# A two-layer hybrid encoder on one core: Gram and attention value products issued in uninterrupted groups, and the bank that the recurrence's chain and its read-out share

## The chip, the cores and the metric

The kernel runs on one core of a Trainium2 chip. The metric is device time in microseconds (us) of one execution; three runs of the kernel before gave 2444.28, 2445.18 and 2440.24 us, with a median of 2444.28 us. The engines are named as the profile names them: PE is TensorE's matmul, PEld its weight load, DVE VectorE, ACT ScalarE, POOL GpSimd and SP SyncE. A line such as L565 is a line of the kernel before; a line of the kernel after is said to be one.

## What is computed

The reference is two layers over a sequence of 1024 frames of width 1024. Layer 0 normalises its input, projects it once, and splits the columns: eight heads of an RWKV-7 recurrence and eight heads of banded attention, whose outputs are joined and projected back. Layer 1 is a convolution module. After each layer stands a squared-ReLU MLP of width 4096. Cut to what the change touches:

```python
def rwkv7_scan(r, decay, k, v, kk, a):          # per head, state S is 64 x 64
    def step(S, inp):
        r_t, w_t, k_t, v_t, kk_t, a_t = inp
        sa = jnp.einsum('bhij,bhj->bhi', S, -kk_t)
        S = S * w_t + sa * (kk_t * a_t) + v_t * k_t      # outer products
        return S, jnp.einsum('bhij,bhj->bhi', S, r_t)
    ...
# then, per head: y normalised, scaled, a bonus added, and times a gate g
    return (y * w + b + bonus) * g

def chunk_band_attention(q, k, v, rel_bias):    # 64-frame chunks, own and 8 previous
    s = einsum('bcqhd,bckhd->bhcqk', qc, kb) * 64 ** -0.5 + bias
    return einsum('bhcqk,bckhd->bcqhd', softmax(s), vb)

x = x + rwkv_attention_mixer(rmsnorm(x), ...)
x = x + sq_relu_mlp(rmsnorm(x), up, down)
```

## The kernel before

**Dense work.** The sequence is worked in two halves of 512 frames. Every large projection runs as split fp32r products of 128x128 by 128x512 (hi times hi, hi times lo, lo times hi), all issued by the helper `dense` at L158. In the mixer's stage these are the input projection of the first half, then of the second half, and then the output projection and the first MLP of the first half.

**The mixer.** Under that dense work lie the recurrence (`rwkv`) and the attention (`attention`), once for each half. The recurrence is worked in units of two heads by 256 frames, cut into four chunks of 64: eight units for each half, 16 in all. A unit goes through three stages, and three units are in flight at once, one in each stage:

- `prep` makes the scaled operands and the Gram products (L565): for each of four chunks and each of the two heads one product with 64 contraction rows, head 0 in rows 0 to 63 and head 1 in rows 64 to 127. The four products of a head fill one bank of tag `w`, of which there are two. L568 masks each bank into `g`. Just ahead, L552 makes the bonus sum in a `w` bank, and L554 reads it into `bv`.
- `stacks` and `invert` transpose and solve (L656, L663, L627, L639), in 64x64 products, in the one bank of tag `v`.
- `chain` carries the state over the four chunks with three dependent products each (L685, L689, L695) and reads the result out (L705, L709), all in the one bank of tag `c`; `finish` normalises it and applies the gate (L460, L467, L731), in the bank `v`.

**The attention.** For two heads and 128 queries, scores (L809, L811), a softmax, transposes of the probabilities (L831, copied to `pT` by ACT at L832), and the value products (L838): for each 128-key tile and each head one product with 64 output columns, accumulated over the key tiles. There are 32 such groups of 2 to 10 products.

**The order.** A scheduler places the instructions of each engine by their estimated readiness and a priority level: support work first, then the recurrence, then the attention, then the dense products. What is issued under the level `run` follows at once. A dense run has one head member at the dense level; the others are tied behind it at level `run`: runs of 6 in the first half of the mixer and of 12 in the second. So a mixer instruction that becomes ready waits for the dense run in hand. Each engine then carries out its own list strictly in order.

An fp32 product that is not a transpose shows up as two matmul records in the profile; a product in fp32r and a transpose show up as one. L565 thus has 256 records for 128 products, and L838 480 for 240.

Of the kernel before, what the change touches and what calls it, by code (L numbers as in the profile page):

```python
# [14 lines left out]
P = 128  # L15
# [47 lines left out]
def encoder_trunk(ctx: ExitStack, tc: tile.TileContext, x, vecs, consts, ext, w2a2, g2, w_in, w_out,  # L63
# [91 lines left out]
    def dense(*a, **k):  # L155
# [9 lines left out]
        runs["n"] += 1  # L165

    def run_of(n):
        runs.update(n=0, size=n)
# [138 lines left out]
    def load_x(h, xrp, out=None):  # L307
# [15 lines left out]
        xs, rhs = [], []  # L323
        st = Stat(pool=out, ps="c")
        for k in range(KT):
# [69 lines left out]
    def rwkv(h, rp, nbuf):  # L395
        keep = {}
        for n, w in (("xdt", C), ("wx", C + 1)):
            t = rp.tile([P, whole(NCH * w)], F32, tag=n, name=n)
            t = keep[n] = t[:, 0 : NCH * w].rearrange("p (c t) -> p c t", t=w)
            nc.gpsimd.memset(t, 0.0)  # L400
        for i in range(2):
            t = keep["xt", i] = rp.tile([P, NCH, 2, C], F32, tag=f"xt{i}", name=f"xt{i}")
            nc.gpsimd.memset(t[:], 0.0)
        units = []
        for tb in range(2 * h, 2 * h + 2):
            units += rwkv_block(tb, rp, nbuf, keep)
        n = len(units)
        for i in range(n + 2):
            gens = []
            if i >= 2:  # L410
                gens.append(units[i - 2][2]())
            if 1 <= i <= n:
                gens.append(units[i - 1][1]())
            if i < n:
                gens.append(units[i][0]())
            while gens:
                for g in list(gens):
                    try:
                        next(g)
                    except StopIteration:  # L420
                        gens.remove(g)

    def rwkv_block(tb, rp, nbuf, keep):
# [28 lines left out]
        def vbank():  # L452
            return psum("v")[:, 0:RT]

        def cbank():
            return psum("c")

# [26 lines left out]
        def prep(hp, u):  # L484
# [68 lines left out]
            bv = rp.tile([P, RT], F32, tag="bv", name="bv", bufs=nbuf)  # L553
            nc.vector.tensor_tensor(out=bv[:], in0=bps, in1=vp[:], op=ALU.mult)  # L554

# [3 lines left out]
            for q4 in range(NCH // 4):  # L559
                mb = [bank(), bank()]  # L560
                for j in range(4):
                    c = 4 * q4 + j
                    for hd in range(2):
                        s = slice(64 * hd, 64 * hd + 64)
                        nc.tensor.matmul(mb[hd][:, j * P : (j + 1) * P], bk[s, c, :], ar[s, c, :],  # L565
                                         start=True, stop=True)
                for hd in range(2):
# [107 lines left out]
        def chain(u):  # L675
# [3 lines left out]
            for hd in range(2):  # L679
                nc.vector.tensor_copy(sv[hs[hd], hd, 0, :], sfin[hs[hd], hp, :])  # L680
            cb = cbank()
            zp, up, sp = cb[:, 0:P], cb[:, 0:C], cb[:, P : 2 * P]
            own = [slice(0, C), slice(C, P)]
# [32 lines left out]
        def finish(u):  # L716
            hp, yc, bv = u["hp"], u["y"], u["bv"]
            sq = e("e3", 2)
            nc.scalar.activation(sq[:], yc[:], AF.Square)
            vq = vbank()  # L720
            rs = head_sums(vq, sq)
# [7 lines left out]
                                           op0=ALU.add, op1=ALU.add)  # L729
            gp = vbank()  # L730
            nc.tensor.matmul(gp, g2s[:, P * hp : P * hp + P], lora_in["sg"][:], start=True, stop=True)  # L731
# [19 lines left out]
    def attention(h, ap):  # L751
# [3 lines left out]
        for hp in range(4):  # L755
# [27 lines left out]
            for qi in range(4):  # L783
# [50 lines left out]
                ob = psum("a")  # L834
                for j in range(nkt):
                    for hd in range(2):
                        cs = slice(hd * C, hd * C + C)
                        nc.tensor.matmul(ob[cs, 0:P], vts[k0 + j][:, cs], pts[hd][:, j * P : (j + 1) * P],  # L838
                                         start=(j == 0), stop=(j == nkt - 1))
                yo = ap.tile([P, P], F32, tag="yo", name="yo", bufs=1)  # L840
# [350 lines left out]
```

## Time and profile before

| | |
|---|---|
| runs | 2444.28, 2445.18, 2440.24 us |
| the profiled execution's own time | 2441.99 us |
| its span | 2440.2 us |
| granted TensorE clock, mean | 0.997 |
| PE busy | 2408.0 us, 99% of the span |
| PEld busy | 1970.2 us, 81% |
| DVE busy | 1710.8 us, 70% |
| ACT busy | 1183.8 us, 49% |
| the mixer's first half on PE, beside projections | about 80 to 470 us |
| the mixer's second half, beside the first MLP | about 490 to 1060 us |

The busy time of PE joins overlapping records, whose ends are modelled. What an instruction costs PE is therefore read from the start of one row of the timeline to the start of the next.

### The profile page before, as it was taken

What the parts mean: (1) busy time and instruction counts of PE and PEld (TensorE: products, weight loads), DVE (VectorE), ACT (ScalarE), POOL (GpSimd) and SP (SyncE); (2) the same over time, 40 slices, a digit from 0 to 9 for tenths busy, and PEclk for the clock granted to TensorE, in tenths of its full rate; (3) what the DMA queues carried; (4) which work ended last, traced back from release to release, by engine and by line L of the source; (5) the groups of instructions that cost most, each with busy time, mean ns of one, the idle gap of its engine ahead of it and who ended that gap; (6) DMA issues with size and microseconds to landing.
All of it is one profiled execution on the core that took longest, in us unless ns stands there. A gap on an engine that the chain in (4) does not pass through costs nothing.

```text
span 2440.2 us, 37269 instructions
## 1 busy us (share of the span) xinstructions
PE 2408.0 (99%) x12972; PEld 1970.2 (81%) x12972; DVE 1710.8 (70%) x3561; ACT 1183.8 (49%) x2282; POOL 113.4 (5%) x251
## 2 busy tenths in 40 slices
PE   8999999999999999999999999999999999999998
PEld 6777777778888888888888888888888888888887
DVE  5688776587677675569999837699997475534434
ACT  5457656666676663443433226434333265423324
POOL 1110101100000000012000000000000000000000
PEclk9999999999999999999999999999999999999999
DMA  8654445543343322363333333433333334333332
GB/s 251 192 152 150 123 113 162 172 133 102 100 121 92 112 72 81 114 185 96 89 102 96 99 100 109 144 96 99 95 99 95 97 109 145 95 100 95 95 97 68
DMA packets 476459, 283.36 MB, mean 116 GB/s; under 512 B 44512, under 2 KB 453472, under 8 KB 476272
## 3 DMA queue, kind: packets, MB, share of 16 engines
q1 hardware_dynamic: 466080, 250.25, 35.5%
q0 software_dynamic: 9152, 29.36, 3.4%
q8 instruction: 102, 1.67, 0.3%
q10 hardware_dynamic: 1040, 1.38, 0.2%
q14 instruction: 85, 0.70, 0.1%
HBM read 247.31 MB, written 36.72 MB: 116 GB/s over the span
## 4 chain that ended last, share of the span: by engine, by line
PE 87%; DVE 4%; DMA 3%; issue 3%; ACT 2%; SPq 0%; POOL 0%; ACTq 0%; DVEq 0%; POOLq 0%
PE d L158 76%; PE w L565 1%; PE a L838 1%; PE v L639 1%; PE a L831 1%; DVE wl L236 1%; PE a L809 1%; PE c L685 1%; PE c L695 1%; DMA xd<-xo 1%; DMA pt<-pd 1%; PE a L811 1%; PE c L689 1%; DMA wr<-in_w_in_dram 0%; PE w L552 0%
## 5 line engine op out<-in xcount | busy, mean ns | idle before, releaser
L235 ACT CAST wh<-wr 128x512 fp32r<-128x512 f32 x744 | 460.3, 620 | 929.0 <-PE d L158 844.3
L158 PE MATMUL d<-xh,wh 128*128 128x512 f32 x1872 | 746.1, 399 | 1.9 <-ACT wh L235 1.3
L158 PE MATMUL d<-xh,wl 128*128 128x512 f32 x1872 | 732.3, 391 | 0.9 <-DVE wl L236 0.9
L158 PE MATMUL d<-xl,wh 128*128 128x512 f32 x1872 | 732.1, 391 | 0.0
L236 DVE TENSOR_TENSOR wl<-wr,wh 128x512 fp32r<-128x512 f32 x744 | 501.6, 684 | 196.8 <-ACT wh L235 143.0
L158 PEld LDWEIGHTS d<-xh,wl 128*128 128x128 f32 x1872 | 352.7, 188 | 77.3 <-DVE wl L236 1.6
L158 PEld LDWEIGHTS d<-xh,wh 128*128 128x128 f32 x1872 | 353.0, 189 | 73.6 <-issue 2.2
L158 PEld LDWEIGHTS d<-xl,wh 128*128 128x128 f32 x1872 | 353.2, 189 | 68.0 <-issue 0.5
L158 PE MATMUL d<-mh,wh 128*128 128x512 f32 (+1 forms) x1040 | 407.2, 392 | 0.0
L158 PE MATMUL d<-mh,wl 128*128 128x512 f32 (+1 forms) x1040 | 402.0, 386 | 0.0
L158 PE MATMUL d<-ml,wh 128*128 128x512 f32 (+1 forms) x1040 | 401.6, 386 | 0.0
L961 DVE SCALAR_TENSOR_TENSOR cv<-u,dwt,cv 128x512 f32<-128x512 f32 x480 | 332.0, 743 | 0.7
L158 PEld LDWEIGHTS d<-mh,wl 128*128 128x128 f32 x1040 | 195.3, 188 | 40.3
L158 PEld LDWEIGHTS d<-ml,wh 128*128 128x128 f32 x1040 | 195.5, 188 | 37.6
L158 PEld LDWEIGHTS d<-mh,wh 128*128 128x128 f32 x1040 | 195.4, 188 | 37.7 <-issue 0.2
L860 DVE TENSOR_TENSOR x<-d,x 128x512 f32<-128x512 f32 (+1 forms) x146 | 97.5, 678 | 153.3 <-PE d L158 152.8
L902 DVE SCALAR_TENSOR_TENSOR t<-d,rstd 128x512 f32<-128x512 f32 x128 | 86.4, 686 | 113.1 <-PE d L158 110.1
L908 DVE TENSOR_TENSOR ml<-t,mh 128x512 fp32r<-128x512 f32 x128 | 87.6, 686 | 14.0 <-ACT mh L906 11.1
L904 ACT ACTIVATE t<-t 128x512 f32<-128x512 f32 x128 | 80.0, 625 | 12.2 <-DVE t L902 11.9
L906 ACT ACTIVATE mh<-t 128x512 fp32r<-128x512 f32 x128 | 78.9, 616 | 0.0
L202 DVE TENSOR_TENSOR acc<-acc,t 128x512 f32<-128x512 f32 (+1 forms) x86 | 57.8, 673 | 11.5 <-ACT t L201 11.1
L694 ACT ACTIVATE sd<-vs,dc 64x64 f32<-64x64 f32 x128 | 44.1, 345 | 38.7 <-DVE vs L698 31.2
(265 smaller groups left out, 2355.6 us busy)
## 6 DMA issues: line engine op xcount, KB each, us to landing
wr<-in_up_dram SPq DMA_DIRECT2D x256, 256.0 KB
wr<-in_dn_dram SPq DMA_DIRECT2D x256, 256.0 KB
wr<-in_w_in_dram SPq DMA_DIRECT2D x104, 256.0 KB
wr<-in_pw_dram SPq DMA_DIRECT2D x96, 256.0 KB
wr<-in_w_out_dram SPq DMA_DIRECT2D x32, 256.0 KB
pd<-t POOLq DMA_DIRECT2D x28, 256.0 KB, 2.7
x<-xd SPq DMA_DIRECT2D x24, 256.0 KB
pt<-pd SPq DMA_DIRECT2D x42, 128.5 KB
```

The costliest lines, as they stand in the source:

```text
L158: ins = nc.tensor.matmul(*a, **k)
L202: nc.vector.tensor_tensor(out=self.acc[:, cols], in0=self.acc[:, cols], in1=sq[:, cols], op=ALU.add)
L235: nc.scalar.copy(hi[:], raw[:])
L236: nc.vector.tensor_tensor(out=lo[:], in0=raw[:], in1=hi[:].bitcast(F32), op=ALU.subtract)
L565: nc.tensor.matmul(mb[hd][:, j * P : (j + 1) * P], bk[s, c, :], ar[s, c, :], start=True, stop=True)
L694: nc.scalar.activation(sd[hs[hd], :], sv[hs[hd], hd, c, :], AF.Copy, scale=dc[hs[hd], c : c + 1])
L860: nc.vector.tensor_tensor(out=xs[m][:, cols], in0=q[:, cols], in1=xs[m][:, cols], op=ALU.add)
L902: nc.vector.scalar_tensor_tensor(out=t[:], in0=q[:], scalar=0.0, in1=rstd[:], op0=ALU.max, op1=ALU.mult)
L904: nc.scalar.activation(sq[:], t[:], AF.Square)
L906: nc.scalar.activation(hi[:], t[:], AF.Square)
L908: nc.vector.tensor_tensor(out=lo[:], in0=sq[:], in1=hi[:].bitcast(F32), op=ALU.subtract)
L961: nc.vector.scalar_tensor_tensor(out=c[:], in0=u[:, tap : tap + T], scalar=dw(tap), in1=c[:], op0=ALU.mult, op1=ALU.add)
```

## The change

It has three parts.

1. The Gram products of a unit are issued through a helper, `Visit`. Its first member carries a wait for the read of the bonus bank (`freed`, the write of `bv`); the seven others are tied behind it at level `run`. The heads alternate from product to product.
2. The attention value products of a group are issued through the same helper. The loop over key tiles and heads runs backwards, so the first product issued is the one whose transposed probabilities come last.
3. The bank of tag `c` is held by one tile for the whole half (`keep["cb"]`). The chain works in one of its first two quarters, by the parity of the head pair, with its three products in the same columns; the read-out and now also `finish` use its second half. The bank `v` is left to `stacks` and `invert`. The statistics of the second half's input go to a bank `v` in place of `c`.

```diff
+    class Visit:
+        def __init__(self, ready=None):
+            self.last, self.ready = None, ready
+
+        def __call__(self, issue, *a, **k):
+            with At("run") if self.last is not None else nullcontext():
+                ins = issue(*a, **k)
+            if self.last is None and self.ready is not None:
+                tc.add_manual_dep(ins.ins, self.ready.ins.name,
+                                  mybir.DependencyInfo(mybir.DependencyClass.Sync, mybir.DependencyReason.DATA),
+                                  reason="a visit begins when its last bank is free")
+            if self.last is not None:
+                tc.add_manual_dep(ins.ins, self.last.ins.name,
+                                  mybir.DependencyInfo(mybir.DependencyClass.NoSync, mybir.DependencyReason.DATA),
+                                  reason="one visit to an array shape")
+            self.last = ins
...
-        st = Stat(pool=out, ps="c")
+        st = Stat(pool=out, ps="v")
...
+        keep["cb"] = psum("c")
...
-            nc.vector.tensor_tensor(out=bv[:], in0=bps, in1=vp[:], op=ALU.mult)
+            freed = nc.vector.tensor_tensor(out=bv[:], in0=bps, in1=vp[:], op=ALU.mult)
...
+                visit = Visit(freed)
                 for j in range(4):
                     c = 4 * q4 + j
                     for hd in range(2):
                         s = slice(64 * hd, 64 * hd + 64)
-                        nc.tensor.matmul(mb[hd][:, j * P : (j + 1) * P], bk[s, c, :], ar[s, c, :],
-                                         start=True, stop=True)
+                        visit(nc.tensor.matmul, mb[hd][:, j * P : (j + 1) * P], bk[s, c, :], ar[s, c, :],
+                              start=True, stop=True)
...
-            cb = cbank()
-            zp, up, sp = cb[:, 0:P], cb[:, 0:C], cb[:, P : 2 * P]
+            cb = keep["cb"]
+            o = P * (hp % 2)
+            zp, up, sp = cb[:, o : o + P], cb[:, o : o + C], cb[:, o : o + P]
...
-            vq = vbank()
+            vq = keep["cb"][:, RT : 2 * RT]
...
-            gp = vbank()
+            gp = keep["cb"][:, RT : 2 * RT]
...
                 ob = psum("a")
-                for j in range(nkt):
-                    for hd in range(2):
+                visit = Visit()
+                for j in reversed(range(nkt)):
+                    for hd in (1, 0):
                         cs = slice(hd * C, hd * C + C)
-                        nc.tensor.matmul(ob[cs, 0:P], vts[k0 + j][:, cs], pts[hd][:, j * P : (j + 1) * P],
-                                         start=(j == 0), stop=(j == nkt - 1))
+                        visit(nc.tensor.matmul, ob[cs, 0:P], vts[k0 + j][:, cs], pts[hd][:, j * P : (j + 1) * P],
+                              start=(j == nkt - 1), stop=(j == 0))
```

How this moves the instructions is seen in PE's own list. In the kernel after, both helpers' products have the line L173; those written to `w` are Gram products, those to `a` value products. Other lines shift: L552, L639, L685, L731, L467, L809 and L811 become L567, L655, L702, L748, L482, L826 and L828. Rows of equal products are joined (x4).

The Gram products of the third unit of the second half, on PE. Before, from the bonus sum L552 on:

```order
L552 MATMUL w<-e,cst 128x256
L565 MATMUL w<-ar,bk 128x128 x4
L685 MATMUL c<-vs,g 128x128
L639 MATMUL v<-xdt,at 64x64 x8
L809 MATMUL a<-kk,qq 128x320
L565 MATMUL w<-ar,bk 128x128 x3
L460 MATMUL v<-cst,e_6493 128x2 x2
L565 MATMUL w<-ar,bk 128x128
L811 MATMUL a<-kk,ql 128x320
```

and in the kernel after, the rows ahead of them (the bonus sum L567 lies two runs of twelve dense products back):

```order
L655 MATMUL v<-e_6477,at 64x64 x8
L482 MATMUL c<-cst,e_6494 128x128 x2
L826 MATMUL a<-kk,qq 128x320
L828 MATMUL a<-kk,ql 128x320
...
L748 MATMUL c<-sg,g2s 128x256
L655 MATMUL v<-e_6503,at 64x64 x8
L173 MATMUL w<-ar,bk 128x128 x8
L702 MATMUL c<-vs,g 128x128
```

Three visits have become one, in alternating heads. Over the whole program the 128 Gram products stand in 43 uninterrupted pieces before and in 16 after.

The value products of a group of six, on PE, before:

```order
L831 MATMUL a<-cst,pt 128x128 x3
L838 MATMUL a<-pT,vt 64x128
L158 MATMUL d<-wh,xh 128x512
L158 MATMUL d<-wh,xl 128x512
L158 MATMUL d<-wl,xh 128x512
...
L689 MATMUL c<-zs,xt_1560 128x64
L838 MATMUL a<-pT,vt 64x128 x5
L809 MATMUL a<-kk,qq 128x512
```

and after, of another group of six:

```order
L848 MATMUL a<-cst,pt 128x128 x3
L158 MATMUL d<-xh,wh 128x512
...
L702 MATMUL c<-vs,g 128x128
L173 MATMUL a<-pT,vt 64x128 x6
L826 MATMUL a<-kk,qq 128x512
L828 MATMUL a<-kk,ql 128x512
```

The single product behind the transposes is gone, and a dense run stands between the last transposes and the group. Over the program the 240 value products stand in 71 pieces before (54 of them of an odd number) and in 32 after, all even. Over all products the array's shape changes from one instruction to the next 393 times before and 271 times after.

The chain and the read-out, on PE, in the first half. Before, the next unit's chain (L685) begins ahead of the gate product L731 of the unit in `finish`:

```order
L460 MATMUL v<-cst,e_2703 128x2 x2
L685 MATMUL c<-vs,g 128x128
L838 MATMUL a<-pT,vt 64x128 x3
...
L467 MATMUL v<-cst,e_2737 128x128 x2
...
L731 MATMUL v<-sg,g2s 128x256
```

and after, it follows it:

```order
L482 MATMUL c<-cst,e_2730 128x128 x2
L643 MATMUL v<-e_2943,g 64x64 x8
...
L748 MATMUL c<-sg,g2s 128x256
L848 MATMUL a<-cst,pt 128x128
...
L702 MATMUL c<-vs,g 128x128
L655 MATMUL v<-xdt,at 64x64 x8
```

The first product of each chain now waits for DVE, which has the gate product's bank to read. The last gate product of the second half stands ahead of 36 dense products of the first MLP before, and ahead of 60 after; that of the first half ahead of 72 dense products of the second input projection before, and of 30 after. The number of products is the same.

More of the change, by code (lines that the diff above doesn't have):

```diff
@@ L453, in vbank @@
             return psum("v")[:, 0:RT]
-        def cbank():
-            return psum("c")
         def head_sums(q, src):
```

## The prediction

> **What bounds the kernel now.** I read the busy table first, then the chain of waits, then the busy time by stretch (the mixer's first half, its turn, its second half, the MLP's end, the rest), and PE's list of waits.
>
> ```profile
> PE 2408.0 (99%) x12972; PEld 1970.2 (81%) x12972; DVE 1710.8 (70%) x3561; ACT 1183.8 (49%) x2282; POOL 113.4 (5%) x251
> PE 87%; DVE 4%; DMA 3%; issue 3%; ACT 2%; SPq 0%; POOL 0%; ACTq 0%; DVEq 0%; POOLq 0%
> 80.00:470.00 390.00, 385.97 (x2710) 304.70 (x2710) 289.98 (x838) 242.85 (x548) 49.25 (x116) 1.00 0.46 138
> 500.00:930.00 430.00, 427.74 (x2957) 350.95 (x2958) 311.02 (x897) 286.72 (x585) 14.40 (x40) 1.00 0.35 100
> PE w L552 <- DVE e L549: 1.0, 3, 0.4
> PE v L731 <- DVE e L644: 0.3, 1, 0.3
> ```
>
> PE is the bound, and in the mixer too: of 390 us of its first half PE idles 4.0, of 430 us of its second 2.3 (first number after the stretch's length), at full clock (1.00); DVE has 100 and 119 us to spare. The list of waits has no row at all for L565 or L838. So what counts is what PE spends on each product, and a shorter product there is a shorter kernel as long as the list stays free of waits. The change leaves the number of products alone, so the question is what the order of products costs. For that I read PE's timeline from the start of one row to the start of the next.
>
> ```profile
> 123.21 0.39 PE L158 MATMUL d<-xl,wh 128*128 128x512 f32 x1
> 123.44 0.39 PE L158 MATMUL d<-xh,wl 128*128 128x512 f32 x1
> 123.76 1.16 PE L565 MATMUL w<-ar,bk 64*128 64x128 f32 x8
> 124.84 0.39 PE L499 MATMUL w<-xl,lora 128*128 128x256 f32 x1
> 625.82 0.48 PE L565 MATMUL w<-ar,bk 64*128 64x128 f32 x2
> 626.24 0.41 PE L811 MATMUL a<-kk,ql 128*128 128x320 f32 x1
> 275.95 0.71 PE L565 MATMUL w<-ar,bk 64*128 64x128 f32 x8
> 276.59 0.43 PE L689 MATMUL c<-zs,xt 128*128 128x64 f32 x2
> 276.96 0.49 PE L565 MATMUL w<-ar,bk 64*128 64x128 f32 x4
> 277.38 0.44 PE L838 MATMUL a<-pT,vt 128*64 128x128 f32 x4
> ```
>
> **The price of a Gram product.** (x8 is four products.) A dense product is followed by the next after 0.23 us (123.21 to 123.44), but by a Gram product, of another array shape, after 0.32: coming in costs 0.09. One lone product holds PE for 0.42 (625.82 to 626.24) and four of one head for 1.08 (123.76 to 124.84): 0.22 for each further one. But four in alternating heads take 0.64 (275.95) and two 0.42 (276.96): 0.22 for each further pair. The second head is free. A visit of eight in alternating heads is then 0.42 + 3 x 0.22 = 1.08.
>
> The price of a value product, read in the same way:
>
> ```profile
> 431.20 0.43 PE L838 MATMUL a<-pT,vt 128*64 128x128 f32 x2
> 431.57 0.50 PE L158 MATMUL d<-xh,wh 128*128 128x512 f32 x1
> 523.60 1.31 PE L838 MATMUL a<-pT,vt 128*64 128x128 f32 x20
> 524.85 0.42 PE L809 MATMUL a<-kk,qq 128*128 128x320 f32 x1
> 277.75 0.38 PE L695 MATMUL c<-vs,bkt 128*128 128x128 f32 x1
> ```
>
> A lone product takes 0.37 us (431.20 to 431.57), a pair also 0.37 (277.38 to 277.75), ten 1.25: 0.22 for each further pair. An odd one costs as much as a pair.
>
> **The sum.** Two group rows give what both lines cost now (busy us, then mean ns):
>
> ```profile
> L838 PE MATMUL a<-pT,vt 128*64 128x128 f32 x480 | 47.2, 284 | 0.1
> L565 PE MATMUL w<-ar,bk 64*128 64x128 f32 x256 | 37.0, 293 | 0.0
> ```
>
> Busy time runs past the start of the next row by about 0.07 a visit (1.16 against 1.08).
> - Gram: 37.0 - 43 x 0.07 = 34.0 us now; 16 x 1.08 = 17.3 after. Gain 16.7. For 27 visits fewer the way in falls away too: 27 x 0.09 = 2.4.
> - Values: 47.2 - 71 x 0.07 = 42.2 now. After, 16 groups of ten and four each of two, four, six and eight: 16 x 1.25 + 4 x (0.37 + 0.59 + 0.81 + 1.03) = 31.2. Gain 11.0, and 39 x 0.09 = 3.5 for the way in.
> - The array's shape changes 122 times fewer, where 27 + 39 visits in and out would be 132: ten more among the other products, 0.9 us back.
>
> Together 16.7 + 2.4 + 11.0 + 3.5 - 0.9 = 32.7 us less on PE. Each of these four readings comes from starts rounded to 0.01; I give the sum 3 us to either side.
>
> **Waits that the change adds.** PE's list is in order, so everything behind a waiting head waits with it: dense runs above all.
> - The head of a Gram visit waits for `bv` (L554), which stands in DVE's list behind the two steps of `finish` (L726, L728):
>
> ```profile
> 856.17 0.70 PE L552 MATMUL w<-e,cst 128*128 128x256 f32 x2 [0.34 <-DVE e L549]
> 864.61 0.48 DVE L726 SCALAR_TENSOR_TENSOR e<-e,vec,v 128x256 f32<-128x256 f32 x1 [1.75 <-PE v L467]
> 865.12 0.48 DVE L728 SCALAR_TENSOR_TENSOR e<-e,vec,bv 128x256 f32<-128x256 f32 x1
> 865.64 0.42 DVE L554 TENSOR_TENSOR bv<-w,vp 128x256 f32<-128x256 f32 x1
> L554 DVE TENSOR_TENSOR bv<-w,vp x16: 396/424/426, 98.9 to 928.3; 128x256 f32<-128x256 f32 x16
> ```
>
> Here `bv` ends 9.9 us after the bonus product began, though it takes 0.42: DVE idles 1.75 until the spread products L467. In the kernel after, the spread (L482) stands a run of twelve, the gate product and mostly a 64x64 visit ahead of the Gram head; twelve dense products alone are 12 x 0.23 = 2.8 us. From the spread's end DVE needs 0.48 + 0.48 + 0.42 = 1.4 us and mostly one or two other operations of up to 0.7. That fits, with little to spare. In the first half six to twelve rows lie between, about 1.8 to 2.9 us, where from the start of L552 to the end of `bv` it took 1.1 to 2.6 before (read unit by unit in the timeline from these two lines).
> - A value group waits for the last `pT` copy. A run of six (1.4 us) or twelve dense products stands between, and before, the first product often followed the transposes at once, for the earlier copy.
> - A chain's head waits for the gate product's reader:
>
> ```profile
> 423.96 0.70 PE L731 MATMUL v<-sg,g2s 128*128 128x256 f32 x2
> 424.70 0.42 DVE L732 TENSOR_TENSOR e<-e,v 128x256 f32<-128x256 f32 x1 [1.00 <-PE v L731]
> ```
>
> The reader ends 1.2 us after the gate product's start; in the list after, 1.5 to 3.9 us of products stand between.
>
> Bounds: nothing less than today, since these lines have no wait in the list. At most, if `bv` is as late as before in all second-half units (1.8 to 14.1 us after the start of the bonus product, in the same reading) and the list after covers only its own products (4 to 12 us at the prices above), three of eight units fall short by 4 to 5 us: 14 us. I take 3, near the lower end, since `bv`'s lateness was DVE waiting for L467, which has moved ahead.
>
> Everything else rides along. Both masks of a unit now follow the visit, but before the second did too. No DMA is added; those behind a finished unit move with it. The conv and MLP stages after 1060 us start earlier and are as before.
>
> **Sum:** 2441.99 - 32.7 + 3 = 2412.3 us for the profiled execution. The median of the runs shown lies 2.3 above it; between the two I forecast **2413 us**, some 1.2% faster.
>
> **The rivals.**
>
> *The mixer's own pace takes the gain.* If the chain of DVE and ACT steps paced the mixer, PE's saving would turn into idle time. The last unit ends close to the end of the dense cover:
>
> ```profile
> 414.63 0.38 PE L685 MATMUL c<-vs,g 128*128 128x128 f32 x2
> 1050.20 0.59 PE L731 MATMUL v<-sg,g2s 128*128 128x256 f32 x2
> 1058.60 0.39 PE L158 MATMUL d<-mh,wl 128*128 128x512 f32 x1
> 1058.83 0.39 PE L158 MATMUL d<-xh,wh 128*128 128x512 f32 x1
> ```
>
> The last gate product is 8.6 us ahead of the next stage (1058.83). And the shared bank puts each chain behind the previous unit's read-out, where it began ahead of its gate product, here by 9.3 us (423.96 less 414.63). If the dense work ran out, the second half would end no earlier: about half the gain is left, 2426 us; in both halves none, 2442. Against it: in the list after, 60 dense products follow the last gate product where 36 did, 14 us of cover, and 30 in the first half, 7 us. [...]
>
> *Alternation does not pay.* Were the free second head seen at 275.95 bound to that place, Gram visits would cost 0.42 + 7 x 0.22 = 1.96 each, 31.4 together, and the gain shrinks by 14.1: 2427 us. Against it: both rows with alternating heads (x8 and x4) say the same.
>
> *The bank wait sits at the head of the list (slower).* The place is the Gram head in the six units from 620 us on. If the lateness of `bv`, 8.5 to 14.1 us there (60 in all), stayed, and only one run of twelve covered it (6 x 2.8 = 17), PE would stall 43 us: 2442 - 33 + 43 = 2452 us. It decides from 33 us on, 5.5 a unit. Against it: two runs and more lie between in four of the six, and `bv`'s lateness had a cause that moved.
>
> **How the numbers follow.** Forecast (2404 to 2419): 0.76. Waits of up to 14 us: 0.08, around 2424. Mixer's pace: 0.05, of which 0.02 leaves a gain. Alternation does not pay: 0.05. The bank wait at full price: 0.03. More gain than forecast: 0.03. A measurement of this kernel can tell about 0.2% (5 us) from no change. Faster: 0.76 + 0.08 + 0.02 + 0.05 + 0.03 = 0.94; the same 0.03; slower 0.03. The range takes 3 us off the sum and 3 for waits that do not come (about 2405), and at the other end the 14 us of waits, and alternation's price: 2404 to 2428.
>
> **What would show it.** In the profile after: L173 products to `w` in 16 rows of x16, each about 1.08 us to the next row's start; products to `a` in 32 rows, x20 at 1.25; PE's busy time in the mixer down by about 33 us and its list of waits with less than 5 us on L173 and L702; the next stage's first dense product near 1029 us in place of 1058.83. Wrong would be a row of waits of over 10 us for DVE `bv` or for L702; a gap between the last gate product and the next stage; or visits of x16 at 2 us.

## The result, and the profile after

The changed kernel takes 2418.6 us (median of four runs, 2417.04 to 2421.22), the kernel before 2444.7 in four runs beside it: ratio 0.9897, 95% interval 0.988 to 0.9915. It is 1.0% faster. The forecast was 2413, its range 2404 to 2428. The profiled execution took 2418.03 us, its span is 2416.3. One execution of one kernel below ran at a granted clock of 0.56 throughout (3959.68 us, where five others took 2433 to 2437) and is left out of its times.

The page of the changed kernel, busy table and shares of the chain of waits by engine:

```profile
PE 2376.4 (98%) x12972; PEld 1954.8 (81%) x12972; DVE 1705.8 (71%) x3561; ACT 1183.8 (49%) x2282; POOL 116.2 (5%) x251
PE 87%; DMA 5%; DVE 4%; ACT 2%; issue 1%; SPq 1%; POOL 0%; ACTq 0%; DVEq 0%; POOLq 0%
```

PE is busy 31.6 us less (2408.0 before). Of the span it idles 39.9 us (2416.3 less 2376.4), where before it idled 32.2 (2440.2 less 2408.0): 7.7 more. The two together, -31.6 + 7.7 = -23.9, are the whole difference of the profiled executions (2441.99 to 2418.03). So the saving came in full, and a quarter of it went to new idle time.

The two groups of products, as the page of the changed kernel groups them (busy us, then mean ns):

```profile
L173 PE MATMUL a<-pT,vt 128*64 128x128 f32 x480 | 33.2, 279 | 0.0
L173 PE MATMUL w<-ar,bk 64*128 64x128 f32 x256 | 18.6, 285 | 0.0
```

The values fell from 47.2 to 33.2, the Gram products from 37.0 to 18.6. PE's timeline after shows a single visit of each kind, and the end of the mixer's second half:

```profile
122.60 1.16 PE L173 MATMUL w<-ar,bk 64*128 64x128 f32 x16
123.69 0.50 PE L158 MATMUL d<-xh,wh 128*128 128x512 f32 x1
...
882.80 1.31 PE L173 MATMUL a<-pT,vt 128*64 128x128 f32 x20
884.05 0.50 PE L158 MATMUL d<-mh,wh 128*128 128x512 f32 x1
...
1020.77 0.59 PE L748 MATMUL c<-sg,g2s 128*128 128x256 f32 x2
1034.84 0.39 PE L158 MATMUL d<-xh,wh 128*128 128x512 f32 x1
```

From start to start a Gram visit takes 1.09 us and a value group of ten 1.25. The next stage begins at 1034.84 in place of 1058.83, 24.0 us earlier; all of the gain is made by then. Its cover, from the last gate product on, is 14.1 us.

Where PE idles is in its list of waits. First two rows of before, then of after those that grew or are new:

```profile
PE w L499 <- ACT e L442: 2.9, 1, 2.9
PE c L689 <- ACT zs L688: 1.2, 4, 0.4
```

```profile
PE c L706 <- ACT zs L705: 4.2, 5, 2.0
PE d L158 <- ACT xh L198: 3.4, 2, 2.6
PE c L702 <- DVE vs L715: 0.6, 2, 0.3
```

L706 is L689 of before: the second product of a chain, which waits for the copy of the first one's result. It rose from 1.2 to 4.2 us. The turn between the halves now stalls on ACT's split of the next stage's input (3.4 us), where before it stalled on `e` (2.9). L173 has no row: neither the bank wait nor the `pT` copies cost anything.

The longest of the chain's stalls, in DVE's and ACT's timeline of the changed kernel and then in PE's:

```profile
297.48 0.37 DVE L609 TENSOR_TENSOR fold<-nb 128x128 f32<-128x128 f32 x1 [1.71 <-DMA nb<-msc]
...
298.87 0.69 DVE L380 TENSOR_TENSOR t<-d,rstd 128x512 f32<-128x512 f32 x1
299.47 0.68 DVE L253 TENSOR_TENSOR wl<-wr,wh 128x512 fp32r<-128x512 f32 x1
300.07 0.21 DVE L704 COPY zs<-c 64x64 f32<-64x64 f32 x1
300.31 0.21 ACT L705 COPY zs<-c 64x64 f32<-64x64 f32 x1 [2.88 <-DVE zs L704]
```

```profile
300.57 0.43 PE L706 MATMUL c<-zs,xt 128*128 128x64 f32 x2 [1.96 <-ACT zs L705]
...
302.17 0.63 PE L158 MATMUL d<-xh,wh 128*128 128x512 f32 x1
302.60 0.63 PE L158 MATMUL d<-xl,wh 128*128 128x512 f32 x1
...
305.24 0.39 PE L158 MATMUL d<-xh,wh 128*128 128x512 f32 x1
305.47 0.40 PE L158 MATMUL d<-xl,wh 128*128 128x512 f32 x1
```

DVE stood 1.71 us at the head of its list for `nb`, the masked blocks coming back from their trip through scratch memory (`g` to `msc` to `nb`, L592 and L597). Behind it stood, among others, a step of the projection, a weight split and the first half of the copy `zs`. The second half is made by ACT, which waited for the first, and PE waited for both. Over the program DVE waits 17.5 us in 12 places for `nb`, against 4.1 in 5 before. And slow clock follows the stall: behind it dense products follow each other after 0.43 us (302.17 to 302.60) and not 0.23 (305.24 to 305.47). The stretches of 10 us show it in the granted clock, the first number behind POOL's count; one stretch of before, two of after:

```profile
490.00:500.00 10.00, 8.80 (x34) 7.06 (x34) 6.90 (x14) 5.71 (x14) 0.19 (x1) 0.83 0.68 203
```

```profile
300.00:310.00 10.00, 9.43 (x81) 7.85 (x82) 7.05 (x33) 6.62 (x17) 1.55 (x3) 0.83 0.45 129
470.00:480.00 10.00, 7.45 (x24) 5.07 (x24) 5.58 (x10) 5.90 (x12) 1.08 (x2) 0.83 0.91 308
```

Between 100 us and the last stage the kernel before has one such dip, after the 2.87 us stall at the turn, and the changed kernel two, behind stalls of 1.96 and 2.55 us. One dip is 10 x (1 - 0.83) = 1.7 us, and it counts as busy.

Over the whole program the trace's record of the granted clock has three dips while PE is busy before (5.1 us) and four after (6.7 us). With them taken off, PE is busy 2402.9 us before and 2369.7 after: 33.2 us less. This is called the busy time at full clock below; it compares the products alone, whatever the clock did in the one execution that was profiled.

### The profile page after: what moved, and what is told of

The parts are those of the page before. It is cut to its first block, busy times and chain, and to the rows that moved or that the text cites. A ratio compares the mean times of both kernels' runs of the same rounds, so it can differ in the third digit from the quotient of the medians.

```text
span 2416.3 us, 37254 instructions
## 1 busy us (share of the span) xinstructions
PE 2376.4 (98%) x12972; PEld 1954.8 (81%) x12972; DVE 1705.8 (71%) x3561; ACT 1183.8 (49%) x2282; POOL 116.2 (5%) x251
## 4 chain that ended last, share of the span: by engine, by line
PE 87%; DMA 5%; DVE 4%; ACT 2%; issue 1%; SPq 1%; POOL 0%; ACTq 0%; DVEq 0%; POOLq 0%
PE d L158 76%; DMA nb<-msc 1%; PE a L173 1%; PE a L848 1%; PE v L655 1%; DVE wl L253 1%; DMA pt<-pd 1%; PE a L826 1%; DMA msc<-g 1%; PE c L712 1%; DMA xd<-xo 1%; PE a L828 1%; DMA xr<-in_x_dram 0%; PE c L706 0%; PE c L702 0%
## 5 line engine op out<-in xcount | busy, mean ns | idle before, releaser
L158 PEld LDWEIGHTS d<-mh,wh 128*128 128x128 f32 x1040 | 195.4, 188 | 37.9 <-issue 0.2
L922 ACT ACTIVATE t<-t 128x512 f32<-128x512 f32 x128 | 80.1, 626 | 14.9 <-DVE t L920 14.6
```

The costliest lines, as they stand in the source:

```text
L158: ins = nc.tensor.matmul(*a, **k)
L922: nc.scalar.activation(sq[:], t[:], AF.Square)
```

## The experiments

### Which part brings the gain

**The shared bank alone.** The products are issued as before:

```diff
-                visit = Visit(freed)
...
-                        visit(nc.tensor.matmul, mb[hd][...], ...)
+                        nc.tensor.matmul(mb[hd][...], ...)
...
-                visit = Visit()
-                for j in reversed(range(nkt)):
-                    for hd in (1, 0):
+                for j in range(nkt):
+                    for hd in range(2):
```

> The shared bank alone; Gram and value products are issued one by one as before. Its list has 46 pieces of Gram products (43 before), 56 of value products (71), 364 changes of shape (393), and the last gate product of the second half stands ahead of 276 dense products (36 before). Theory of prices (PE pays 0.20 us + 0.09 for each visit, and 0.22 for each pair): 3 x 0.29 - 15 x 0.24 - 12 x 0.11 = -4.0 us, so about 2440 us, with waits as before. Rival, the shared bank brings the new waits of the chain's second product on ACT (4.2 us in the changed kernel against 1.2): 2443 to 2447 us, with a row of 3 us or more for that wait.

Measured: 2441.32 us (ten runs), ratio 0.9997 [0.9987, 1.0006]: no difference. But the order is another one: the last gate product of the second half now stands ahead of 276 dense products (36 before), that of the first ahead of 132 (72). The mixer is finished earlier, and with PE full all the same that is worth nothing by itself. At full clock PE is busy 2399.5 us, 3.4 less than before, near the 4.0 of the expectation; idle time is 33.2 us (32.2 before).

**The Gram visits and the shared bank**, value products as before (the second half of the diff above).

> The changed kernel without the visits of value products. The list has 16 Gram visits, 53 pieces of value products (36 odd), 302 changes of shape. Theory of prices: Gram -19.1, value products -18 x 0.24 - 18 x 0.11 = -6.3, so -25 us on PE; with 7 us of added waits as in the changed kernel 2427, with none 2420 us. Rival, alternation is only cheap where it was seen: 2434 or more.

Measured: 2420.52 us (2418.69 to 2422.79), ratio 0.991 [0.9895, 0.9925]; 20.8 us below the shared bank alone; the prediction's terms for the Gram products are 19.1 (16.7 + 2.4). At full clock PE is busy 2378.9 us, 20.6 less than with the bank alone.

**The value visits and the shared bank**, Gram products as before (the first half of that diff).

> The changed kernel without the visits of Gram products. The list has 32 visits of value products, 48 pieces of Gram products, 321 changes of shape. Theory of prices: value products -14.5, Gram 5 x 0.29 = +1.5, so -13 us on PE: 2432 us without added waits. If the waits of the changed kernel come from the Gram visits (behind their head everything waits), they are missing here and the time is 2430 to 2433; if they come from the shared bank or the value visits, 2436 to 2440.

Measured: 2433.61 us (median of five executions, 2433.15 to 2436.72), ratio 0.9967 [0.9955, 0.998], between the two ranges expected; its trace is of the execution left out, so only its times are used. That is 7.7 us below the shared bank alone, where the prediction's terms for the values were 14.5. Part of the difference was gone before: with the bank alone the value products already stand in 56 pieces (42 odd) and not in 71 (54 odd), and at the prices of the expectations (0.24 us a piece, 0.11 for an odd one) 24 x 0.24 + 42 x 0.11 = 10.4 us were left. Added on top of the Gram visits, the value visits bring 2 us (2420.5 to 2418.6), which is within the spread of the runs. The busy table of the kernel before this one (Gram visits and bank) tells where the rest went:

```profile
PE 2380.6 (98%) x12972; PEld 1955.7 (81%) x12972; DVE 1707.7 (71%) x3561; ACT 1184.8 (49%) x2284; POOL 113.1 (5%) x251
```

Its profiled execution has one dip of the clock, the changed kernel's four. At full clock the value visits thus save 9.2 us of PE (2378.9 less 2369.7), as the prices have it (53 pieces, 36 odd: 21 x 0.24 + 36 x 0.11 = 9.0). Of that, 5.0 goes back as slow clock and 2.0 as idle time (39.9 against 37.9 us). The number of dips differs from one execution to the next: the mean clock of this kernel's four runs from 0.997 to 0.999, of the changed kernel's four from 0.996 to 0.997.

**Both visits, without the shared bank:**

```diff
-        keep["cb"] = psum("c")
...
-            cb = keep["cb"]
-            o = P * (hp % 2)
-            zp, up, sp = cb[:, o : o + P], cb[:, o : o + C], cb[:, o : o + P]
+            cb = cbank()
+            zp, up, sp = cb[:, 0:P], cb[:, 0:C], cb[:, P : 2 * P]
...
-            vq = keep["cb"][:, RT : 2 * RT]
+            vq = vbank()
...
-            gp = keep["cb"][:, RT : 2 * RT]
+            gp = vbank()
```

> Both kinds of visits, without the shared bank. PE's list costs as much as that of the changed kernel at the same prices (16 and 32 visits, 278 changes of shape), but the last gate product of each half stands behind the last dense product (0 in cover, against 30 and 60): two chain products, the read-out and the finish of the last unit have nothing beside them. Theory of prices alone: as the changed kernel, 2416 to 2421 us. Theory of the mixer's pace: the uncovered tail, some 8 to 12 us of dependent steps in the second half and one or two in the first, is added: 2427 to 2433 us, with PE idle just ahead of the next stage. Should the waits of the changed kernel be the shared bank's, 5 us of that come off.

Measured: 2442.08 us (ten runs), ratio 0.9993 [0.9983, 1.0003], 9 us above the higher of the two expectations. The gain is gone, though PE's products stand in visits as in the changed kernel. The busy table of this kernel, a slice at the end of its second half, and PE's timeline there:

```profile
PE 2388.0 (98%) x12972; PEld 1958.2 (80%) x12972; DVE 1710.7 (70%) x3561; ACT 1182.1 (48%) x2280; POOL 102.3 (4%) x251
```

```profile
1050.00:1060.00 10.00, 7.45 (x53) 6.17 (x54) 3.29 (x9) 4.69 (x13) 0.19 (x1) 0.56 0.22 67
```

```profile
1050.91 0.57 PE L713 MATMUL c<-vs,bkt 128*128 128x128 f32 x2 [2.12 <-ACT vs L709]
...
1058.45 0.69 PE L484 MATMUL v<-cst,e 128*128 128x128 f32 x2 [1.00 <-ACT e L482]
1059.71 1.22 PE L749 MATMUL v<-sg,g2s 128*128 128x256 f32 x2 [0.57 <-DVE e L744]
1060.37 0.99 PE L158 MATMUL d<-xh,wh 128*128 128x512 f32 x1
1061.15 0.63 PE L158 MATMUL d<-xl,wh 128*128 128x512 f32 x1
```

The dense work has run out: the last step of the last unit's chain, the read-out and the gate product stand bare, with waits in between, and the clock granted falls to 0.56. Over the program PE idles 53.8 us (span 2441.8 less 2388.0), 13.9 more than in the changed kernel, and is busy 11.6 us longer with the same products: 8.2 of it is slow clock, and 3.4 is there at full clock too. The two longest stretches of slow clock, 13.7 us each, begin at 474 and 1051 us, where the two halves end. The added idle time is not all there: 3.9 us fall about the end of the first half (300 to 510 us) and 3.1 about that of the second (1030 to 1065), but 5.3 in the second half ahead of its end, where dense products still follow. So the loss is idle time, in part in places that lost their cover, and slow clock, most of it at these two places. This is the prediction's first rival, but with the shared bank as its remedy and not its cause.

### What a visit is worth

**Heads one after the other within the Gram visit:**

```diff
-                for j in range(4):
-                    c = 4 * q4 + j
-                    for hd in range(2):
+                for hd in range(2):
+                    for j in range(4):
+                        c = 4 * q4 + j
```

> The changed kernel with the loops of a Gram visit turned round: four products of head 0, then four of head 1, in the same 16 uninterrupted visits (272 changes of shape, 271 in the changed kernel). Theory of prices: a visit of eight costs 0.42 + 7 x 0.22 = 1.96 us, less one free overlap where the heads meet, against 1.08; 16 x 0.8 = +11 to +14 us, so 2430 to 2433 us where the changed kernel takes 2418.6. Rival, only the number of changes of shape counts: 2418 to 2421 us.

Measured: 2426.64 us (2424.35 to 2427.13), ratio 0.9932 [0.9917, 0.9947]: 8.0 us more than the changed kernel, between the two expectations. Its group row, and one visit in its timeline:

```profile
L173 PE MATMUL w<-ar,bk 64*128 64x128 f32 x256 | 27.4, 285 | 0.0
```

```profile
98.74 1.71 PE L173 MATMUL w<-ar,bk 64*128 64x128 f32 x16
100.38 0.68 PE L679 MATMUL v<-cent,vp 64*64 64x64 f32 x16
```

A visit takes 1.64 us and not 1.09; sixteen visits make 8.8, and the group row has 8.8 (27.4 less 18.6). The alternation is what pays, but the price with it undone is 1.64, where the prediction's second rival had 1.96.

**The Gram visit without the bank wait at its head** (`Visit()` in place of `Visit(freed)`). The order then puts the first product ahead of the bank wait, and each visit breaks in two: one product, and later seven.

> The changed kernel without the wait for the bonus bank's reader at the head of a Gram visit; the second product still needs that bank. The list falls back to 32 pieces of Gram products and 314 changes of shape. Theory of prices: 16 more pieces x 0.29, and most of the first pieces without the other head beside them, +6 to +10 us: 2425 to 2429 us. Theory that the head's wait itself stalls PE: faster than the changed kernel, under 2416 us.

Measured: 2426.24 us (2425.2 to 2427.03), ratio 0.9932 [0.9917, 0.9947], inside the first expectation; the group row has 26.2. The added wait on `bv` is worth 7.6 us. It costs nothing itself (no row in the changed kernel's list of waits), and it holds the visit together: in this kernel the lone product takes 0.41 us and the seven behind it 1.08, as much as all eight together.

**Value products forward**, first key tile first, so that the first product issued is the one whose probabilities come first:

```diff
-                for j in reversed(range(nkt)):
-                    for hd in (1, 0):
+                for j in range(nkt):
+                    for hd in range(2):
```

> The changed kernel with the value products in the order of before (first key tile and head 0 first), still tied together. The list has 43 pieces of value products (22 odd) in place of 32, and 297 changes of shape. Theory of prices: 11 x 0.24 + 22 x 0.11 and 4 more changes = +5 us, 2424 us. If the members behind the head also stall the list for later copies of the probabilities (they are tied behind the first), 2428 us or more, with PE waiting for ACT at the value products. If the order does not matter, 2417 to 2420 us.

Measured: 2427.27 us (2426.04 to 2428.53), ratio 0.9936 [0.9919, 0.9952], between the first two expectations. The groups are split again, 43 pieces, 22 of them odd, and the row rises from 33.2 to:

```profile
L173 PE MATMUL a<-pT,vt 128*64 128x128 f32 x480 | 38.3, 280 | 0.0
```

That is 5.1 of the 8.7 us. At the prediction's 0.09 us each, 26 more changes of shape (297 against 271) are 2.3, and the profiled execution has one dip of the clock more, 1.7. Idle time is the same (40.0 against 39.9 us), and no wait for a `pT` copy shows here either.

### Where the 7.7 us of idle time come from

The stretch that the prediction showed for the first half, in the changed kernel:

```profile
80.00:470.00 390.00, 379.50 (x2751) 306.70 (x2750) 290.19 (x842) 246.17 (x554) 51.69 (x122) 0.99 0.49 145
```

PE idles 10.5 us there where it idled 4.0 before: 6.5 of the 7.7 us lie in the first half. The turn idles 3.4 us in place of 3.5 (470 to 510 us), and 1.6 are added in the second half. By parts, idle time is 33.2 us with the bank alone, 37.9 with the Gram visits added and 39.9 in the changed kernel (one profiled execution each).

**Half of the scratch stores on POOL's queue.** The four blocks of a head's `g` are stored by SP and POOL in turn, to shorten the round trip:

```diff
-                    nc.sync.dma_start(msc[hd, 4 * b : 4 * b + 4, :, :]...
+                    (nc.gpsimd if b % 2 else nc.sync).dma_start(msc[hd, 4 * b : 4 * b + 4, :, :]...
```

> The changed kernel with half of the eight stores of the masked blocks (from g to the scratch buffer) issued on POOL's queue, the other half on SP's as before. In the changed kernel DVE waits 17.5 us for the load that follows these stores (4.1 us before the change), and the chain's copies queue behind that wait. If that round trip causes the added waits of PE, DVE's wait for the load falls to under 9 us, PE's waits in the mixer fall by 3 to 6 us, and the time is 2413 to 2416 us. If the added waits come from elsewhere, 2418 to 2420 us with the list of PE's waits as in the changed kernel.

Measured: 2417.91 us (2412.53 to 2419.22), ratio 0.9894 [0.9879, 0.9909], not to be told from the changed kernel. The profiled execution is the fastest of the four; it has one dip of the clock where the changed kernel's has four (5.0 us), and idles 1.2 us less. DVE's and PE's waits of this kernel:

```profile
DVE fold L609 <- DMA nb<-msc: 11.8, 10, 3.3
```

```profile
PE v L643 <- DVE e L637: 4.1, 4, 2.2
```

DVE's wait falls by a third, from 17.5 to 11.8, and the stall on `c` behind `zs` leaves the head of PE's list; a stall of the same size stands in `invert` (L643). Nor does a long wait of DVE for `nb` always reach PE: with the Gram visits and the bank it is 16.8 us, and PE waits only 0.9 us for `zs` at L706.

**The changed kernel once more**, beside the two that follow.

> The changed kernel itself, beside the next two on one chip: 2417 to 2421 us.

Measured: 2419.11 us (2416.57 to 2420.3), ratio 0.9904 [0.9891, 0.9918]. The result repeats.

**All of those stores on POOL's queue.**

> The changed kernel with all eight stores of the masked blocks on POOL's queue. The last gate product of a half stands ahead of 72 and 192 dense products (30 and 60 in the changed kernel). Moving half of them took a third off DVE's wait for the load behind them (17.5 to 11.8 us), but PE then waited for the second round trip through scratch (4.1 us at the first solve product, 0.4 in the changed kernel), and the time hardly moved. If each round trip in turn paces the first half, this one too gives 2415 to 2419 us, with PE's waits moved to the solve's products and not gone. If the store is the cause, 2411 to 2414 us.

Measured: 2425.78 us (2421.75 to 2431.72), ratio 0.9935 [0.9922, 0.9948]: slower than either expectation. DVE's wait for `nb` is 20.6 us, longer than with all stores on SP, and PE idles 47.5 us, 7.6 more than in the changed kernel; why is not shown.

**Two queues, and dense runs of 8 in the first half** (`RUN = 8, 12, 8` for `6, 12, 6`).

> Stores on two queues, and dense runs of 8 in place of 6 in the first half (12 in the second as before). Each dependent step of the first half gets 0.46 us more of dense cover; the last gate products stand ahead of 80 and 204 dense products, so the tail stays covered. If PE's added waits come from too little cover for steps whose length is set by DVE, ACT and the round trips, waits in the first half (21 us over the prices between 100 and 450 us in the changed kernel, 14 before the change) fall to 14 or less and the time is 2409 to 2414 us. If not, 2415 to 2420 us.

Measured: 2443.49 us (eleven runs), ratio 1.0002 [0.9993, 1.0011]. Both expectations missed by over 20 us: all of the gain is lost. The list of products is hardly dearer (1.5 us at full clock). Its busy table, PE's timeline at the end of the first half and the stretch of time there:

```profile
PE 2388.1 (98%) x12972; PEld 1965.2 (80%) x12972; DVE 1710.1 (70%) x3561; ACT 1189.6 (49%) x2284; POOL 147.0 (6%) x315
```

```profile
447.29 0.43 PE L706 MATMUL c<-zs,xt 128*128 128x64 f32 x2 [0.55 <-ACT zs L705]
448.27 0.49 PE L712 MATMUL c<-vs,bkt 128*128 128x128 f32 x2 [0.55 <-ACT vs L708]
449.43 0.49 PE L702 MATMUL c<-vs,g 128*128 128x128 f32 x2 [0.68 <-DVE vs L715]
```

```profile
453.00:472.00 19.00, 16.00 (x93) 12.97 (x90) 5.49 (x20) 8.41 (x18) 1.50 (x4) 0.50 0.02 7
```

Here too the mixer stands bare: between 441 and 467 us no dense product stands between the steps of the last unit's chain, each step shows its latency, and 19 us run at half the clock. And yet 80 dense products follow the last gate product, as the expectation had counted: they all stand behind the chain and its read-out, where they cover nothing of it. PE idles 55.8 us (2443.9 less 2388.1) and is busy 11.7 us longer than in the changed kernel, 10.2 of it slow clock: the picture of the kernel without the shared bank at the end of its first half, by another edit. (A stall of 5.8 us at about 80 us, on `xl`, is in it too.)

**Runs of 3 in the first half** (`RUN = 3, 12, 6`), the opposite step.

> The changed kernel with dense runs of 3 in place of 6 beside the first half's mixer (RUN = 3, 12, 6); nothing else. It asks where the waits of the first half come from that the prediction left out. Theory A: with fewer pieces in PE's list a ready step of the mixer waits longer for its place, and the mixer falls behind the dense work that covers it; shorter runs give it places back, as longer runs took them (runs of 8: 2443). Then: the price of PE's list rises by 0.6 us (281 changes of shape against 271), 147 dense products stand between the first half's last gate product and the next stage against 90, the stalls on c behind ACT zs go, the granted clock has no dip between 90 and 470 us, and the time is 2409 to 2416 us. Theory B: the waits are fixed latencies of DVE, ACT and the scratch round trip, whatever the runs: waits as in the changed kernel, PE's list 0.6 us dearer, 2417 to 2422 us.

Measured: 2422.78 us (2419.56 to 2424.93), ratio 0.9919 [0.9906, 0.9933]. The time is just above the second expectation, but the trace shows what the first one named. PE's waits in this kernel, and two stretches of it:

```profile
PE w L514 <- ACT wh L252: 6.1, 1, 6.1
PE c L706 <- ACT zs L705: 1.0, 3, 0.5
```

```profile
90.00:300.00 210.00, 206.10 (x1559) 162.39 (x1558) 181.13 (x510) 138.09 (x302) 23.43 (x56) 1.00 0.48 142
300.00:480.00 180.00, 176.64 (x1203) 139.71 (x1203) 117.12 (x347) 118.00 (x271) 27.69 (x64) 1.00 0.54 164
```

The stall on `c` behind `zs` is down from 4.2 to 1.0 us, the clock has no dip between 90 and 480 us, and PE idles 7.3 us there. In the changed kernel it idles 13.1 in the same stretches (14.9 in its second profile):

```profile
90.00:300.00 210.00, 203.47 (x1469) 163.19 (x1467) 170.13 (x467) 129.06 (x281) 23.63 (x56) 1.00 0.49 145
300.00:480.00 180.00, 173.48 (x1264) 140.29 (x1265) 118.25 (x372) 116.23 (x269) 28.11 (x64) 0.98 0.51 155
```

So the waits are no fixed latencies: they depend on how often PE's list opens to the mixer. The mixer also runs ahead: 219 dense products follow the first half's last gate product, 30 in the changed kernel (the expectation's 147 and 90 are not these counts). The time did not follow, for two reasons. This kernel stalls 6.1 us at about 80 us on a weight split (the place where the changed kernel waits 2.0 for `xl`), so that idle time over the program is 41.1 us against 39.9; why the split is late there is not shown. And at full clock PE is busy 5.6 us longer, where both theories had 0.6 for the ten more changes of shape; what the other 5 are is not shown.

## Why the prediction was right, and where it was not

**The bound, and the sum on PE: right.** 32.7 us less were forecast; busy time fell by 31.6, one extra dip of the clock (1.7 us) included, and by 33.2 at full clock. Values 33.2 - 32 x 0.07 = 31.0 us against 31.2 worked out, Gram 18.6 - 16 x 0.07 = 17.5 against 17.3.

**The three waits that were named: right, at nothing.** `bv`, `pT` and the chain's head cost 0, 0 and 0.6 us in the changed kernel, and the 0.6 is for the chain's own state (`vs`), not for the gate product's reader. With the value products as before, one wait for `bv` of 1.5 us appears; the slower rival's 43 us are far off.

**The step that failed is "I take 3" for the added waits, with "Everything else rides along".** The idle time rose by 7.7 us, and none of the three waits priced is in it: it is the middle of the chain (L706, 1.2 to 4.2 us) and small stalls elsewhere, 6.5 us of it in the first half. Dense runs of 3, which add openings to PE's list, took 5.8 us of idle time out of that half; runs of 8 lost 25 us. That the openings move these waits is shown. That the visits bring the waits by closing openings (one long piece stands where two or three were, so steps ready in between come later) is argued only: the idle time comes with the Gram visits (33.2 to 37.9 us), but cutting each Gram visit in two did not bring it down (41.2). Nor was it told apart from a plainer cause: with 33 us less of products, PE has less work to hide the same steps of DVE and ACT behind. The 3 us that softened the miss were meant for waits that did not come, so that much is luck. The scratch round trip is shown as the cause of one stall (300.57) and no more: DVE's wait for `nb` was cut by a third, and the time stayed.

**The reading of the shared bank had the wrong sign.** The prediction gave it only a cost, the chain behind the read-out. Without it the visits gain nothing. The runs have 2442.08 us without sharing against 2418.6 with it. Sharing alone does not tell the two kernels apart: `finish` shares a bank in both, with `stacks` and `invert` before and with the chain after, and the prediction looked at one side of that only. What sharing frees is the bank `v`, which only `stacks` and `invert` use then. That this is why the mixer runs ahead (276 dense products behind the last gate product with the bank alone, none with the visits alone) is argued from the order; no run gave `finish` a third bank to prove it. The 60 and 30 products of cover in the changed kernel were counted in the prediction, but as an effect of the whole change: it did not ask which part made them.

**Alternation: right in kind, its loss too dear.** The rival's 1.96 us a visit is 1.64, and undoing it costs 8.0 us and not 14.1.

**The signs that were named.** Sixteen rows of x16 at 1.08: 1.09. x20 at 1.25: 1.25. Waits under 5 us on L173 and L702: 0.6. The next stage near 1029: 1034.84, late by the 5.7 us by which the profiled execution missed its 2412.3. Idle time is 4.7 of it (7.7 less 3) and PE's busy time 1.1, by rounding 0.1 too much; without the extra dip the busy time would have fallen by more than was forecast.

## What to carry to other kernels

Where the array's shape changes often, read from start to start what one product, a pair and a visit cost: here 128 products in 16 visits in place of 46 gave 21 us. But longer dense runs in an in-order list take places from the steps that depend on each other, and the gain hangs on the cover of the last of them: count the dense products between the last unit's dependent steps and behind them, before and after and for each part of the change alone. The count behind the last step is not enough: in the kernel with runs of 8 it was 80, and the chain ahead of it stood bare. To compare two traces, take the slow clock out of the busy time first. A stall is to be priced with the slow clock behind it: 1.7 us here, behind the stalls of 1.96, 2.55 and 2.87 us, and none behind the one of 2.19 with two store queues.

## What the runs showed of the hardware

**Behind windows in which PE idled 1.9 us or more, the granted clock was half for 3.41 us in the traces before and after.** Their record of the granted clock has three and four slow stretches while PE works. Each is 3.41 us long, and within one execution they begin whole multiples of 3.41 us apart: at 55.79, 79.69 and 492.70 us before, at 55.65, 79.55, 301.41 and 475.49 us after. For the reading here, time is cut from these starts into windows of that length. The changed kernel's stall of 1.96 us (up to 300.57) lies inside one window, and the next one is slow; dense products follow there at 0.43 us in place of 0.23. In the kernel with two store queues a longer stall, of 2.19 us, is split over two windows of that length, and the clock stays full (1.00). The changed kernel's two windows, then the other kernel's stall and its two (PE's busy time is the number behind the length, the clock stands behind POOL's count):

```profile
298.00:301.41 3.41, 1.45 (x12) 0.99 (x11) 3.16 (x14) 0.32 (x2) 0.57 (x2) 1.00 0.51 152
301.41:304.82 3.41, 3.41 (x12) 2.83 (x11) 2.07 (x11) 1.90 (x6) 0.51 (x1) 0.50 0.54 153
```

```profile
305.66 0.68 PE L643 MATMUL v<-e,g 64*64 64x64 f32 x16 [2.19 <-DVE e L637]
301.09:304.50 3.41, 2.38 (x12) 1.84 (x10) 1.68 (x6) 2.76 (x9) 0.00 (x0) 1.00 0.26 62
304.50:307.91 3.41, 2.25 (x36) 1.86 (x36) 2.71 (x8) 1.50 (x5) 0.00 (x0) 1.00 0.30 85
```

PE idles 1.96 us in the first of these windows, and 1.03 and 1.16 in the last two. From 25 us to PE's last product, the traces before and after have seven windows at full clock in which PE idled 1.9 us or more (1.92 to 2.63), and each was followed by half the clock (twice behind PE's last product); of the windows followed by full clock none had more than 1.40. Two more slow stretches began behind windows with less idle time, 1.51 us before and 1.03 after; what brought those is not shown. So of two stalls of some 2 us the shorter was followed by 1.7 us of slow clock and the longer by none. That the place of a stall in the windows decides this is the author's reading of these traces; no run moved a stall to prove it.

**Gram products of the two heads in alternation cost less than one head after the other.** Eight in alternating heads (contraction rows 0 to 63 and 64 to 127) took 1.09 us in the changed kernel, four and four of one head 1.64; in the prediction's rows a further product of the same head added 0.22 us (four in 1.08, one in 0.42), and one of the other head nothing (two in 0.42).

**Two edits that hardly change the price of PE's list (3.4 and 1.5 us) cost the whole gain**, about 25 us each: 13.9 and 15.9 us as idle time, 8.2 and 10.2 as slow clock.
